# A transformer block on one core: the causal mask of diagonal score units added by a matmul instead of VectorE

## The chip, the core and the metric

The kernel runs on one core of one Trainium2 chip. The metric is device time in microseconds (us) of one execution. The engines are TensorE (PE; PEld is its weight load), VectorE (DVE), ScalarE (ACT), GpSimd (POOL) and SyncE (SP, whose queue issues most DMAs).

## The reference

One layer over 2048 positions of width 1024: RMSNorm, a joint projection, a gated mixing branch (A), forgetting attention (B), the output projection, and a feed-forward part with a causal convolution. What the change touches is branch B, 8 heads of dimension 64:

```python
def block(args):
    i, qi, ci = args
    s = jnp.einsum('bhtd,bshd->bhts', qi, k, preferred_element_type=jnp.float32) * scale
    s = s + ci[..., :, None] - c[:, :, None, :]
    qpos = i * Q_BLOCK + jnp.arange(Q_BLOCK)
    s = jnp.where(kpos[None, :] <= qpos[:, None], s, -jnp.inf)
    p = jax.nn.softmax(s, axis=-1)
    return jnp.einsum('bhts,bshd->bthd', p.astype(v.dtype), v)
...
x = x + jnp.concatenate([out_a, out_b], axis=-1) @ w_out[l]
x = x + conv_ffn(rms_norm(x, norm_ffn_g[l]), w_up[l], w_conv[l], b_conv[l], w_down[l])
```

`c` is a cumulative sum of log-sigmoid forget logits. Arithmetic is at float32 accuracy: operands are split in a high and a low fp32r part, and a product is three matmuls.

## The kernel before

Two kinds of work run side by side. The first is the chain of large products, in 512-column tiles: the input projections in two halves of 1024 positions (`a_half`), the output projection of the first half (`c_half`), its up-projection (`d_half`), the output projection of the second half (`c_late`), and then the feed-forward products of the rest (`up_mms`, L1171 to L1173, and `down`, L1373). Up to `c_late` each tile `mm` is a series of 24 matmuls, all at L212 in `mm3`, with `thi`, `tlo` the activations' parts and `whi`, `wlo` the weights'.

The second is attention, a generator (`b_stream`) that is advanced once every few L212 matmuls (`tick`, `RATES`). It goes over 4 query blocks `tb` of 512 and within each over 8 heads `h`. For each pair a first pass (`b_max`, L774 to L784) forms scores and reduces them on VectorE to a maximum per query (`part`), and a second pass (`b_mix`) forms them again, transposed, by unit `sc` of 128 keys: two matmuls into a PSUM tile `s` or `dn` (L821 with keys `m1` and queries `t1`, L822 with `m2` and `t2`), an exponential on ScalarE into `e` (L827), its high part `ph` on ScalarE (L832) and low part `pl` on VectorE (L833), the running sum on VectorE (L835), and two or three units later the product with the values (L809 with `ph`, L810 with `pl`, into `o`). A pair has 4*tb + 4 units. The last 4 are diagonal: unit j of them covers query columns from 128*j on (widths 512, 384, 256, 128), and its first 128 columns get the mask `maskT` on VectorE (L825). After a pair of heads, L851 sums `sum` over the keys, L852 inverts it, `rw` (L857) spreads it, four transposes (L186, `s<-ident,rw`) turn it, L860 scales, and the result goes to DRAM (`mixh`, `mixl`).

`need(tb)` makes the program finish query block tb before the DMAs `thi<-mixh`, `tlo<-mixl` (`load_mix`) bring it to `c_half` or `c_late`: the last chunks of the second projection block of each half (from L212 matmul 2304 of the trace's count in the first half, from 4800 in the second; 36 further ones can run without the last chunks) wait for it. Transposes L186 `dn<-ident,ar` turn rows of the first half for the up-projection.

The order of instructions on every engine is not the order of the code. A scheduler of the framework places each instruction in a simulated run of its own, with priorities (`high_priority` for attention's steps, weights' casts further ahead), so an instruction more or less in attention moves others on all engines. The pools' buffer counts are in `BUFS`: three `s` tiles and, later, two `dn` for scores, two `m2` and `v`, one `t2`.

Of the kernel before, what the change touches and what calls it, by code (L numbers as in the profile page):

```python
# [10 lines left out]
BF16 = mybir.dt.bfloat16  # L11
AF = mybir.ActivationFunctionType
ALU = mybir.AluOpType
# [5 lines left out]
P = 128  # L19
# [6 lines left out]
TB = 512  # L26
EPS = 1e-6
BIG = 1e30
EVEN = 104

# [21 lines left out]
def f32(ap):  # L54
    return ap.bitcast(F32)
# [26 lines left out]
class Block:  # L82
# [589 lines left out]
    def b_consts(self):  # L672
        nc, bp = self.nc, self.bp
        ones = self.til(self.sp, [P, TB], F32, "st")[:2, :]
        nc.gpsimd.memset(ones, 1.0)
        for i in range(2):
            self.dma(self.ones_d[:, i * TB:(i + 1) * TB], ones)
        for k in self.kx:
            self.dma(k[:, 128:130, :], self.ones_d.unsqueeze(0).broadcast_to([8, 2, HALF]))
        self.mask = bp.tile([P, TB], BF16, name="mask")  # L680
        nc.gpsimd.memset(self.mask, 0.0)

        nc.gpsimd.affine_select(out=self.mask, in_=self.mask, compare_op=ALU.is_ge, fill=BIG, base=384,
                                pattern=[[-1, TB]], channel_multiplier=1)

        self.maskT = bp.tile([P, P], BF16, name="maskT")
        bp.tile([P, EVEN], F32, name="even")
        nc.gpsimd.memset(self.maskT, 0.0)
        nc.gpsimd.affine_select(out=self.maskT, in_=self.maskT, compare_op=ALU.is_ge, fill=BIG, base=0,
                                pattern=[[1, P]], channel_multiplier=-1)  # L690

        self.rowsel = bp.tile([8, 4, P], BF16, name="rowsel")
        nc.gpsimd.memset(self.rowsel, 1.0)
        for base, mult in ((0, 1), (1, -1)):
            nc.gpsimd.affine_select(out=self.rowsel, in_=self.rowsel, compare_op=ALU.is_ge, fill=0.0, base=base,
                                    pattern=[[-2 * mult, 4], [0, P]], channel_multiplier=mult)
        self.M1, self.T1 = [[self.til(self.mp, [P, TB], F32R, tag) for _ in range(2)] for tag in ("m1", "t1")]
        for m in self.M1:
            nc.gpsimd.memset(f32(m[64:128, :]), 0.0)
            nc.gpsimd.memset(f32(m[96:104, :]), 1.0)  # L700
        for t in self.T1:
            nc.gpsimd.memset(f32(t[64:128, :]), 0.0)
            self.dma(f32(t[66:68, :]), self.ones_d[:, 0:TB])
# [95 lines left out]
    def b_mix(self, h, tb, t1, t2, turn):  # L799

        nc, bp, pp = self.nc, self.bp, self.bpp
        po = self.til(pp, [P, TB], F32, "o")
        total = self.til(self.mp, [P, TB], F32, "sum")
        ns = 4 * tb + 4
        late = []

        def pv():
            sc, c, v, ph, pl = late.pop(0)
            nc.tensor.matmul(po[:, c], lhsT=v, rhs=ph[:, c], start=sc == 0, stop=False)  # L809
            nc.tensor.matmul(po[:, c], lhsT=v, rhs=pl[:, c], start=False, stop=sc == ns - 1)  # L810

        for sc in range(ns):
            if sc == TURN and turn:
                turn()
            if sc % 4 == 0:
                m1, m2, v4 = self.b_keys(h, sc // 4, True)
            j = max(0, sc - 4 * tb)
            c = slice(j * P, TB)
            ks = slice((sc % 4) * P, (sc % 4 + 1) * P)
            ps = self.scores([P, TB])  # L820
            nc.tensor.matmul(ps[:, c], lhsT=m1[:, ks], rhs=t1[:, c], start=True, stop=False)  # L821
            nc.tensor.matmul(ps[:, c], lhsT=m2[:, ks], rhs=t2[:, c], start=False, stop=True)  # L822
            if sc >= 4 * tb:
                d = ps[:, j * P:(j + 1) * P]
                nc.vector.tensor_tensor(d, d, self.maskT, op=ALU.add)  # L825
            e = self.room([P, TB], F32, "e") if sc else total
            nc.scalar.activation(e[:, c], ps[:, c], AF.Exp, scale=-1.0)  # L827
            if len(late) >= (LAG + 1 if self.more else LAG):
                pv()
            ph = self.room([P, TB], F32R, "ph")  # L830
            pl = self.room([P, TB], F32R, "pl")
            nc.scalar.activation(ph[:, c], e[:, c], AF.Copy)  # L832
            nc.vector.tensor_tensor(pl[:, c], e[:, c], f32(ph[:, c]), op=ALU.subtract)  # L833
            if sc:
                nc.vector.tensor_tensor(total[:, c], total[:, c], e[:, c], op=ALU.add)  # L835
            late.append((sc, c, v4[:, sc % 4, :], ph, pl))
            yield
        while late:
            pv()
            yield  # L840

        if h % 2 == 0:
            self.op = self.til(self.mp, [P, TB], F32, "op")
            self.rr = self.til(bp, [P, 4, 2], F32, "rr")
        op = self.op
        own, other = (slice(0, 64), slice(64, 128)) if h % 2 == 0 else (slice(64, 128), slice(0, 64))
        nc.scalar.activation(op[own, :], po[other, :], AF.Copy)
        nc.vector.tensor_tensor(op[own, :], po[own, :], op[own, :], op=ALU.add)
        ps = self.scores([P, 4])
        for i in range(4):  # L850
            nc.tensor.matmul(ps[:, i:i + 1], lhsT=total[:, i * P:(i + 1) * P], rhs=self.mhalf[:, 0:1], start=True, stop=True)  # L851
        nc.vector.reciprocal(self.rr[:, :, h % 2], ps)  # L852
        if h % 2 == 0:
            return

        rw = self.til(self.mp, [P, 4, 2, 64], F32, "rw")
        nc.scalar.activation(rw, self.rr.unsqueeze(3).broadcast_to([P, 4, 2, 64]), AF.Copy, scale=-0.5)  # L857
        yield
        pr = self.transpose4(None, "s", [rw[:, i, :, :].rearrange("p a b -> p (a b)") for i in range(4)])
        nc.vector.tensor_tensor(op, pr, op, op=ALU.mult)  # L860
        oh = self.room([P, TB], F32R, "ph")
        ol = self.room([P, TB], F32R, "pl")
        self.split_sb(op, oh, ol)
        cs = slice(512 + (h - 1) * 64, 512 + (h + 1) * 64)
        self.dma(self.mixh[tb][cs, :], f32(oh))
        self.dma(self.mixl[tb][cs, :], f32(ol))
# [692 lines left out]
```

## Time and profile before

| | |
|---|---|
| median of 3 runs | 2424.99 us (2424.58 to 2426.9) |
| the profiled execution | 2425.66 us, of which the span from first to last instruction is 2424.0 us |
| mean granted clock of TensorE | 0.991 |
| PE busy | 2375.0 us (98%), 11224 matmuls |
| PEld, DVE, ACT, POOL busy | 81%, 78%, 47%, 14% |
| attention | from 142.9 us (first L774) to about 1518 us |

A row of a group has the line, engine, operation, out<-in, shapes and count; then busy us, mean ns of one; then the engine's idle time ahead of it and who ended it. A row of the timeline has start, duration (us), engine, line, operation and what ended idle time in brackets. A row of waits has the total, the number and the longest. Matmuls are pipelined, so the duration of one (0.39 us for 512 columns) is longer than the step from its start to the next one's (0.22 to 0.23).

### The profile page before, as it was taken

Reading aid. Unit: us, or ns where it says so; the run is one execution under the profiler, and the core shown is the slowest. Engines: PE = TensorE matmul, PEld = TensorE weight load, DVE = VectorE, ACT = ScalarE, POOL = GpSimd, SP = SyncE. Lnnn points to the kernel's source line nnn. Section 1 sums busy time; section 2 is a strip of 40 time slices with the busy share of each in tenths; the row PEclk is TensorE's granted clock in tenths of the full one; section 3 lists DMA queues with packets and bytes.
Section 4 is the critical chain, followed back from the end, with each engine's and each line's share of the span. In section 5 each row is a group of like instructions: output and inputs, shape, how many; then the busy total and the mean of one; then the engine's idle time right before and its main releaser. Section 6 shows DMA issues by size and latency. Waiting matters only on the chain.

```text
span 2424.0 us, 32411 instructions
## 1 busy us (share of the span) xinstructions
PE 2375.0 (98%) x11224; PEld 1974.9 (81%) x11224; DVE 1900.7 (78%) x3324; ACT 1150.2 (47%) x1986; POOL 335.8 (14%) x315
## 2 busy tenths in 40 slices
PE   9999999999999999999999999899999999999998
PEld 7888888988778888888887887688888887888887
DVE  5357777866679988999999887598888877957875
ACT  4235655432424444454454435465555455454444
POOL 4114130101123222222222010100000000000001
PEclk9999999999999999999999999899999999999999
DMA  8663536658545444444444453312222228538633
GB/s 263 185 242 99 176 95 175 173 170 294 174 156 195 163 143 152 144 155 148 150 159 151 164 200 132 122 53 88 86 79 87 87 91 308 163 100 299 202 119 123
DMA packets 234517, 379.56 MB, mean 157 GB/s; under 512 B 49944, under 2 KB 109464, under 8 KB 232928
## 3 DMA queue, kind: packets, MB, share of 16 engines
q1 hardware_dynamic: 229312, 353.36, 45.3%
q0 software_dynamic: 5040, 24.12, 2.5%
q8 instruction: 89, 1.46, 0.3%
q14 instruction: 76, 0.62, 0.1%
HBM read 283.82 MB, written 93.72 MB: 156 GB/s over the span
## 4 chain that ended last, share of the span: by engine, by line
PE 83%; DVE 6%; DMA 5%; issue 3%; ACT 1%; POOL 1%; SPq 0%; POOLq 0%; DVEq 0%; ACTq 0%
PE mm L212 39%; PE D L1373 14%; PE A L1171 3%; PE A L1172 3%; PE A L1173 3%; PE o L810 2%; PE o L809 2%; PE s L774 2%; PE s L822 2%; PE s L821 2%; PE B L1172 2%; PE B L1173 2%; PE B L1171 2%; DVE sum L835 1%; PE C L1171 1%
## 5 line engine op out<-in xcount | busy, mean ns | idle before, releaser
L212 PE MATMUL mm<-tlo,whi 128*128 128x512 f32 x896 | 352.4, 394 | 0.0
L212 PE MATMUL mm<-thi,whi 128*128 128x512 f32 x896 | 351.9, 393 | 0.5 <-DVE vn L520 0.5
L212 PE MATMUL mm<-thi,wlo 128*128 128x512 f32 x896 | 352.0, 393 | 0.0
L212 PE MATMUL mm<-whi,thi 128*128 128x512 f32 (+2 forms) x768 | 279.3, 364 | 16.3 <-DMA thi<-mixh 9.0
L212 PE MATMUL mm<-wlo,thi 128*128 128x512 f32 (+2 forms) x768 | 277.3, 362 | 2.0 <-DVE wlo L165 2.0
L212 PE MATMUL mm<-whi,tlo 128*128 128x512 f32 (+2 forms) x768 | 275.8, 360 | 0.4 <-DMA tlo<-mixl 0.4
L151 POOL TENSOR_SCALAR whi<-raw 128x1024 fp32r<-128x1024 f32 (+3 forms) x114 | 144.3, 1267 | 915.0 <-PE mm L212 743.0
L212 PEld LDWEIGHTS mm<-thi,whi 128*128 128x128 f32 x896 | 168.6, 188 | 34.5 <-issue 0.7
L212 PEld LDWEIGHTS mm<-tlo,whi 128*128 128x128 f32 x896 | 168.6, 188 | 33.6
L212 PEld LDWEIGHTS mm<-thi,wlo 128*128 128x128 f32 x896 | 168.6, 188 | 33.1
L212 PEld LDWEIGHTS mm<-whi,thi 128*128 128x128 f32 x768 | 146.9, 191 | 37.6 <-DMA thi<-mixh 10.0
L835 DVE TENSOR_TENSOR sum<-sum,e 128x512 f32<-128x512 f32 (+3 forms) x249 | 161.7, 650 | 13.6 <-ACT e L827 10.6
L212 PEld LDWEIGHTS mm<-wlo,thi 128*128 128x128 f32 x768 | 147.2, 192 | 22.5 <-DVE wlo L165 2.9
L212 PEld LDWEIGHTS mm<-whi,tlo 128*128 128x128 f32 x768 | 146.7, 191 | 21.8 <-DMA tlo<-mixl 1.3
L165 DVE TENSOR_TENSOR wlo<-raw,whi 128x1024 fp32r<-128x1024 f32 (+2 forms) x106 | 131.5, 1241 | 33.7 <-POOL whi L151 33.4
L827 ACT ACTIVATE e<-s 128x512 f32<-128x512 f32 (+3 forms) x207 | 105.2, 518 | 108.5 <-DVE s L825 46.9
L1373 PE MATMUL D<-wl,xh 128*128 128x512 f32 x368 | 141.5, 389 | 0.0
L1373 PE MATMUL D<-wh,xh 128*128 128x512 f32 x368 | 140.8, 389 | 0.2 <-DVE xo L1474 0.2
L833 DVE TENSOR_TENSOR pl<-e,ph 128x512 fp32r<-128x512 f32 (+3 forms) x195 | 123.5, 637 | 21.1 <-PE o L810 13.9
L1373 PE MATMUL D<-wh,xl 128*128 128x512 f32 x368 | 137.7, 389 | 0.0
L832 ACT ACTIVATE ph<-e 128x512 fp32r<-128x512 f32 (+3 forms) x195 | 105.4, 549 | 46.1 <-PE o L809 39.1
L931 ACT ACTIVATE a<-mm 128x512 f32<-128x512 f32 x88 | 52.6, 598 | 122.3 <-PE mm L212 118.3
(1837 smaller groups left out, 5756.4 us busy)
## 6 DMA issues: line engine op xcount, KB each, us to landing
raw<-in_w_up_dram SPq DMA_DIRECT2D x72, 512.0 KB
m<-kx SPq DMA_DIRECT2D x160, 136.0 KB
x<-act SPq DMA_DIRECT2D x84, 256.0 KB
m<-kx SPq DMA_DIRECT2D x67, 256.0 KB
v<-vd SPq DMA_DIRECT2D x67, 256.0 KB
raw<-in_w_in_dram SPq DMA_DIRECT2D x28, 512.0 KB
raw<-in_w_out_dram SPq DMA_DIRECT2D x24, 512.0 KB
tw<-in_w_down_dram SPq DMA_DIRECT2D x11, 1024.0 KB
```

The lines of the kernel that those rows point to most:

```text
L151: self.cast_ins = self.nc.gpsimd.tensor_scalar(out, in_, 1.0, 0.0, ALU.mult, ALU.add).ins
L165: nc.vector.tensor_tensor(lo, raw, f32(hi), op=ALU.subtract)
L212: self.last_mm = self.nc.tensor.matmul(ps, lhsT=a[k], rhs=b[k], start=i == 0, stop=i == 3 * n - 1).ins
L827: nc.scalar.activation(e[:, c], ps[:, c], AF.Exp, scale=-1.0)
L832: nc.scalar.activation(ph[:, c], e[:, c], AF.Copy)
L833: nc.vector.tensor_tensor(pl[:, c], e[:, c], f32(ph[:, c]), op=ALU.subtract)
L835: nc.vector.tensor_tensor(total[:, c], total[:, c], e[:, c], op=ALU.add)
L931: nc.scalar.activation(a[:, 2:TB + 2], ps, AF.Copy)
L1171: mm(ps, lhsT=xh[:, ks], rhs=yh[:, k, :], start=fresh and k == 0, stop=False, **kw)
L1172: mm(ps, lhsT=xh[:, ks], rhs=yl[:, k, :], start=False, stop=False, **kw)
L1173: mm(ps, lhsT=xl[:, ks], rhs=yh[:, k, :], start=False, stop=k == 3, **kw)
L1373: nc.tensor.matmul(bank[t], lhsT=x[i][:, ts], rhs=w[k], start=fresh and j == 0 and i + k == 0, stop=last and i == 1, **kw)
```

## The change

The mask of a diagonal unit is added inside the accumulation: between L821 and L822 a matmul with a bfloat16 unit matrix `same` as weights and the bfloat16 `maskT` as moving operand adds it to the unit's first 128 columns of PSUM. The VectorE addition is gone. `same` is made once, by a ScalarE copy of `ident` that stands at the head of ScalarE's order. The padding tile `even` shrinks by as many bytes as `same` takes, so other tiles keep their addresses.

```diff
-EVEN = 104
+EVEN = 40
...
+        self.same = bp.tile([P, P], BF16, name="same")
+        nc.scalar.activation(self.same, self.ident, AF.Copy)
...
             nc.tensor.matmul(ps[:, c], lhsT=m1[:, ks], rhs=t1[:, c], start=True, stop=False)
+            if sc >= 4 * tb:
+                nc.tensor.matmul(ps[:, j * P:(j + 1) * P], lhsT=self.same, rhs=self.maskT, start=False, stop=False,
+                                 skip_group_check=True)
             nc.tensor.matmul(ps[:, c], lhsT=m2[:, ks], rhs=t2[:, c], start=False, stop=True)
-            if sc >= 4 * tb:
-                d = ps[:, j * P:(j + 1) * P]
-                nc.vector.tensor_tensor(d, d, self.maskT, op=ALU.add)
```

In the new program lines behind the edits stand a little lower: the two score matmuls, L821 and L822, are L824 and L828 there, the mask L826, the value products, L809 and L810, are L812 and L813, and L774 and L851 are L777 and L854.

Three places show how the scheduler's order moves. All are TensorE's rows.

The first is a head of query block 1, late in it, whose second pass begins. Before, its first two units (tiles `s_5194`, `s_5210`) follow close behind the end of the head ahead, L822 right behind L821:

```order
L821 MATMUL s_5194<-t_49_401,m_48_400 128x512
L810 MATMUL o_4946<-pl_5091,v_5059 128x384
L809 MATMUL o_4946<-ph_5117,v_5059 128x256
L821 MATMUL s_5210<-t_49_401,m_48_400 128x512
L822 MATMUL s_5210<-t_1174_5185,m_1177_5190 128x512
L822 MATMUL s_5194<-t_1174_5185,m_1177_5190 128x512
L212 MATMUL mm_6854<-wlo_6550,thi_6158 128x512
```

Now the head starts earlier against the L212 matmuls, and 28 of these stand between a third L821 and the L822 of all three units:

```order
L813 MATMUL o_4948<-pl_5141,v_5061 128x128
L824 MATMUL s_5236<-t_49_403,m_48_402 128x512
L212 MATMUL mm_6437<-wlo_6342,thi_6161 128x512
...
L212 MATMUL mm_6492<-wlo_6342,thi_6161 128x512
L828 MATMUL s_5212<-t_1174_5187,m_1177_5192 128x512
L828 MATMUL s_5196<-t_1174_5187,m_1177_5192 128x512
L828 MATMUL s_5236<-t_1174_5187,m_1177_5192 128x512
```

Further loads of L212 work thus stand ahead of the first matmul that needs `t2`, `m2` of the new head.

The second is the end of query block 1. Before, the last values products, the `rw` transposes, other transposes and the first-pass scores of block 2 stand in one piece of 46 rows without an L212, right after the last L212 that can run without block 1:

```order
L809 MATMUL o_5187<-ph_5354,v_5277 128x128
L186 MATMUL dn_7144<-ident,ar_6647 128x128
...
L810 MATMUL o_5187<-pl_5355,v_5277 128x128
L186 MATMUL s_5435<-ident,rw_5421 128x128 x4
L774 MATMUL s_6351<-m_48_400,t_50_402 128x512
L774 MATMUL s_6359<-m_48_400,t_50_402 128x512
L186 MATMUL dn_7171<-ident,ar_6647 128x128
```

Now the same transposes come 57 L212 matmuls ahead of that point, and L212 rows follow at once:

```order
L813 MATMUL o_5189<-pl_5357,v_5279 128x128
L186 MATMUL s_5437<-ident,rw_5423 128x128 x4
L777 MATMUL s_6353<-m_48_402,t_50_404 128x512
L777 MATMUL s_6361<-m_48_402,t_50_404 128x512
L212 MATMUL mm_6856<-whi_6551,thi_6160 128x512
L212 MATMUL mm_6856<-wlo_6552,thi_6160 128x512
```

So block 1 ends earlier against the products, and what stood in one piece stands between them.

The third is the end of attention. Before, 85 matmuls of attention in one piece, units of the last two heads, follow the last L212 that can run without block 3; they begin with

```order
L212 MATMUL mm_15131<-whi_14875,tlo_14853 128x512
L810 MATMUL o_12972<-pl+_3050_13172,v+_3034_13116 128x512
L809 MATMUL o_12972<-ph+_3055_13193,v_13183 128x512
L821 MATMUL dn_13334<-t_49_401,m_48_400 128x512
L822 MATMUL dn_13334<-t_3076_13291,m_3079_13296 128x512
```

Now it is 17, the last products and sums of the last head alone:

```order
L212 MATMUL mm_15133<-whi_14877,tlo_14855 128x512
L813 MATMUL o_13295<-pl+_3143_13518,v_13461 128x512
L812 MATMUL o_13295<-ph+_3148_13538,v_13528 128x512
...
L812 MATMUL o_13295<-ph+_3163_13597,v_13528 128x128
L854 MATMUL s_13625<-mhalf,sum_13296 128x1
L813 MATMUL o_13295<-pl+_3164_13598,v_13528 128x128
L186 MATMUL dn_13636<-ident,rw_13631 128x128 x4
L212 MATMUL mm_15087<-whi_14883,thi_14853 128x512
```

The units that were in that piece now stand between earlier L212 rows. On SP's queue the loads of attention keep their sequence within a head but move with it.

## The prediction

> **What bounds the kernel now.** I read the page's busy times and its chain first, then the waits of TensorE (PE), then a table of stretches.
>
> ```profile
> PE 2375.0 (98%) x11224; PEld 1974.9 (81%) x11224; DVE 1900.7 (78%) x3324; ACT 1150.2 (47%) x1986; POOL 335.8 (14%) x315
> PE 83%; DVE 6%; DMA 5%; issue 3%; ACT 1%; POOL 1%; SPq 0%; POOLq 0%; DVEq 0%; ACTq 0%
> PE mm L212 <- DMA thi<-mixh: 9.0, 2, 7.2
> PE o L810 <- DVE pl L833: 4.0, 6, 1.2
> PE s L822 <- DMA v<-vd: 3.2, 1, 3.2
> PE s L774 <- DVE part L777: 2.9, 4, 1.0
> 625.00:641.00 16.00, 12.79 (x52) 10.35 (x51) 5.11 (x13) 5.83 (x13) 4.03 (x6) 0.79 0.73 215
> 641.00:655.00 14.00, 14.00 (x71) 11.62 (x70) 9.19 (x18) 7.72 (x14) 1.86 (x3) 1.00 0.62 190
> 655.00:680.00 25.00, 19.14 (x81) 12.56 (x80) 18.96 (x40) 7.22 (x14) 0.00 (x0) 0.80 0.35 107
> 900.00:1200.00 300.00, 298.84 (x1371) 247.72 (x1370) 275.90 (x522) 140.47 (x258) 67.08 (x54) 1.00 0.46 151
> 1495.00:1515.00 20.00, 17.78 (x66) 10.73 (x66) 18.01 (x35) 16.84 (x32) 0.00 (x0) 0.91 0.17 54
> 1515.00:1532.00 17.00, 8.40 (x32) 6.31 (x32) 4.72 (x10) 10.16 (x15) 3.49 (x8) 0.60 0.50 181
> ```
>
> TensorE is 98% busy and 83% of the chain, so what it gains or loses is the time. The waits say where it is not full: few places, and the long ones are singles. The stretches (columns: span, PE, PE weight loads, DVE, ACT, POOL, granted clock, DMA share, GB/s) show them. In 641 to 655 us PE is full, 71 matmuls in 14 us at clock 1.00. In 625 to 641, 655 to 680 and from 1495 it has fewer matmuls and clocks of 0.60 to 0.91: these are the places where the first product stream (`mm`, L212) has run into data that attention has not delivered. Elsewhere, as in 900 to 1200 us, PE is 99.6% busy and VectorE (DVE) 92%.
>
> **The cost: 128 more matmuls.** There are 32 pairs of head and query block with 4 diagonal units each: 128. Each unit gets a 128-column matmul and its weight load between L821 and L822. Such a bfloat16 matmul stands nowhere in this trace. The nearest rows are the 128-column matmuls among 512-column ones:
>
> ```profile
> 641.50 0.39 PE L212 MATMUL mm<-whi,tlo 128*128 128x512 f32 x1
> 641.72 0.22 PE L809 MATMUL o<-ph,v 128*128 128x128 f32 x1
> 641.78 0.45 PE L212 MATMUL mm<-whi,thi 128*128 128x512 f32 x1
> 642.07 0.22 PE L810 MATMUL o<-pl,v 128*128 128x128 f32 x1
> ...
> 649.18 0.22 PE L821 MATMUL s<-t,m 128*128 128x128 f32 x1
> 649.24 0.27 PE L822 MATMUL s<-t,m 128*128 128x128 f32 x1
> 649.35 0.45 PE L212 MATMUL mm<-whi,thi 128*128 128x512 f32 x1
> 649.63 0.39 PE L212 MATMUL mm<-wlo,thi 128*128 128x512 f32 x1
> ```
>
> The durations overlap, so starts are what counts. From 641.50 to 641.72 a 512-column matmul takes its 0.22 to 0.23 us. The short one at 641.72 is followed after 0.06, but the next long one then takes 0.29 (641.78 to 642.07): short and long together 0.35, so the short one costs 0.12. Where two short ones stand together (649.18 to 649.63, 0.45 us with the long one) the second adds 0.10. I take 0.115 us each, wide or narrow unit: 128 x 0.115 = 14.7 us. The low end is the 0.06 alone: 7.7 us. The high end is a matmul that overlaps nothing, its full 0.22: 28.2 us. I stay with 14.7 because the disturbed neighbour after it is again an fp32r one, as in these rows. The Trainium skill, "TensorE: Matmul & The Clock Gate", section on the back-to-back issue gap, gives about 81 ns for each 128-column matmul with its weight load; by that the sum would be 10.4 us.
>
> **What goes.** VectorE loses 128 additions:
>
> ```profile
> L825 DVE TENSOR_TENSOR s<-s,maskT x108: 277/290/332, 160.8 to 1508.8; 128x128 f32<-128x128 f32 x108
> L825 DVE TENSOR_TENSOR dn<-dn,maskT x20: 279/286/293, 952.3 to 1506.6; 128x128 f32<-128x128 f32 x20
> ```
>
> 128 x 0.29 = 37 us of VectorE, nearly all beside a full PE: worth nothing directly. It shortens the way from scores to exponential on diagonal units, since ScalarE no longer queues behind VectorE's backlog. The one copy that makes `same` stands ahead of ScalarE's first split and I cost it at nothing: if ScalarE's work there were late, it would be one copy, under 0.3 us.
>
> **What moves, and why I expect a gain.** The order on every engine changes from the first diagonal unit on; the pieces ahead of this section show that attention stands earlier against L212. That matters at three places.
>
> Place 1, about 631 us:
>
> ```profile
> 631.32 0.40 PE L821 MATMUL s<-t,m 128*128 128x512 f32 x1
> 634.92 1.19 PE L822 MATMUL s<-t,m 128*128 128x512 f32 x2 [3.21 <-DMA v<-vd]
> ...
> 640.18 0.41 PE L212 MATMUL mm<-whi,tlo 128*128 128x512 f32 x1
> ```
>
> PE starts nothing between 631.32 and 634.92, where 0.23 was due: 3.4 us. Then 12 matmuls (2 of L822, 10 of L212) take until 640.18, 5.26 us instead of 12 x 0.23 = 2.8: 2.5 us at the low clock. Together 5.9. In the new order 28 matmuls of L212 stand ahead of this head's first L822, 6.4 us of cover against a wait of 3.2. I count all of it, 5.9.
>
> Place 2, the end of query block 1:
>
> ```profile
> 654.78 0.38 PE L186 MATMUL dn<-ident,ar 128*128 128x128 f32 x2
> ...
> 660.70 0.66 PE L186 MATMUL s<-ident,rw 128*128 128x128 f32 x4 [0.17 <-ACT rw L857]
> ...
> 673.98 0.79 PE L212 MATMUL mm<-whi,thi 128*128 128x512 f32 x1 [1.87 <-DMA thi<-mixh]
> ```
>
> ```profile
> L774 PE MATMUL s<-m,t 96*128 96x512 f32 x12 | 6.7, 598 | 1.8 <-DVE part L777 1.7
> L186 PE MATMUL dn<-ident,ar 128*128 128x128 f32 x27 | 4.2, 277 | 0.4 <-DVE tlo L196 0.3
> ```
>
> The second fence has the two largest groups of that stretch: 12 first-pass scores and 27 transposes, beside which only some 20 rows of L212 stand. Of all matmuls that start between 655 and 680 us, 34 have 512 columns (34 x 0.23 = 7.8 us), 29 are transposes at 0.11 apart (from 654.78: two end 0.38 after the first start, one lasts 0.27; 3.2 us) and 15 are narrower (3 of 384, 3 of 256, the rest shorter, about 1.7 us): 12.7 us of work in 25, 12.3 lost. Here all L212 work that needs no result of block 1 is used up before the last heads' tail, and transposes and first-pass scores then queue behind VectorE. In the new order 57 matmuls of L212 follow the `rw` transposes before the first that needs the last chunks: 13 us of full PE. At the end of attention, in the rows of place 3, the same way from `rw` to L212 takes 8.3 us (1517.79 to 1526.09). So it is covered; I count 11, keeping 1.3 for the slow part that has other causes.
>
> Place 3, the end of attention:
>
> ```profile
> 1508.79 0.29 DVE L825 TENSOR_TENSOR s<-s,maskT 128x128 f32<-128x128 f32 x1
> ...
> 1514.98 0.31 PE L810 MATMUL o<-pl+_3164_13596,v 128*128 128x128 f32 x1
> ...
> 1517.79 1.12 PE L186 MATMUL dn<-ident,rw 128*128 128x128 f32 x4 [1.22 <-ACT rw L857]
> 1526.09 0.79 PE L212 MATMUL mm<-whi,thi 128*128 128x512 f32 x1 [7.18 <-DMA thi<-mixh]
> ```
>
> Between 1495 and 1515 us PE starts 65 matmuls, 45 of them wide (10.4 us), 4 of 384 and 4 of 256 (1.2), 12 shorter (0.7): 12.3 of 20, 7.7 lost to the pace of VectorE (18.0 of 20 busy). Before, 85 attention matmuls follow the last L212 that can run without the result; now 17 do, the rest stand between L212 rows. Four of the removed additions lie here as well, those of the last head's diagonal units, the last at 1508.79: 1.2 us. The last head is still worked off one unit after another, so I count 5 of the 7.7. The tail after 1514.98 stays: nothing in the new order covers the 7.2 us for the last `thi`.
>
> New waits in a denser order, and small waits that the lighter VectorE saves, I let cancel but for 1 us of new ones: the four rows of waits above other than the named stops amount to a few us in all.
>
> **Sum.** 14.7 - 5.9 - 11 - 5 + 1 = -6.2 us, and with the rounding of the low clock at place 3 (PE enters the final wait at full clock, so the 1.2 us of L851 and L186 there shrink) about -7.5. The profiled execution took 2425.66 us (span 2424.0 and 1.7 around it), 0.7 above the median of the three runs, 2424.99. I predict 2417.5 us.
>
> **Rivals.** (a) Only place 2 is repaired: a load is late elsewhere in place of that at 631, and the last head again runs at VectorE's pace. For it: SP's order of loads moves as well, and the cover of head 7's first L822 is as short in the new order as before. Then 14.7 - 11 - 1 = +2.7: 2428, no difference that can be told.
> (b) Slower: PE is the full engine, it gets 14.7 us more, and the stops re-form, because they come from one mechanism, VectorE's rate: each unit asks it for a difference and a sum, and a new order does not change that. Then only the four additions and part of place 1 are won, about 3: 2437. It decides when less than 9.8 us of the 24 lost at the three places come back (14.7 less the 4.9 that are 0.2%, what a measurement of this kernel can tell from no change). Against it: VectorE is idle 6.0 of the 25 us of place 2 (18.96 busy), so that stop is order, not rate. The Trainium skill, "Perfetto Trace Analysis", optimization strategy, says to work on the most contended engine, and by that rule moving work onto PE loses; the trace agrees that PE is that engine, but also shows it waiting.
> (c) The short matmul costs 0.06 only: 7 us less than the forecast, 2410.5.
>
> **Chances.** Forecast 0.58 (own range 2410 to 2422), (a) 0.22, (b) 0.12, (c) 0.08. The range reaches from (c) with place 3 whole, 2408, over (a) to 2431, which leaves out (b) and the high price. Faster by over 0.2%, below 2420.1: nine tenths of the forecast and (c), 0.61. Within 0.2%: 0.27. Slower: 0.12.
>
> **What would show it.** Right: the waits of L822 on a DMA (3.2) and of L774 on `part` (2.9) go, that on `thi` falls from 9.0 in 2 to about 7 in 1; the stretch of 25 us at clock 0.80 near 660 us is full; the run of attention alone before 1518 us is short; a masked unit's L821 to the matmul after L822 takes 0.115 us longer. Wrong: start to start steps of 0.2 us around the mask matmul, or PE waits on `e`, `pl` and loads scattered from 150 to 1500 us that amount to over 5 us.

## The result and the profile after

The changed kernel takes 2422.64 us (median of 20 runs, 2418.44 to 2425.25) against 2425.18 for the kernel before (20 runs). The ratio is 0.9986, interval 0.998 to 0.9993: 0.14% faster, or 1.7 to 4.9 us. The interval lies wholly below 1, so the gain is real, but it is under the 0.2% that the prediction took as the bound of a difference. The time lies inside the predicted range (2408 to 2431), 5 us above the predicted 2417.5: a third of the forecast gain of 7.5 us came. The profiled execution took 2422.66 us, with a span of 2420.9.

From the page, busy times and chain, and from the waits of TensorE (total, number, longest, us):

```profile
PE 2379.3 (98%) x11352; PEld 1973.2 (82%) x11352; DVE 1881.9 (78%) x3196; ACT 1152.9 (48%) x1987; POOL 331.3 (14%) x315
PE 79%; DVE 5%; DMA 2%; issue 2%; ACT 2%; POOL 1%; SPq 0%; POOLq 0%; DVEq 0%; ACTq 0%
PE mm L212 <- DMA thi<-mixh: 8.8, 2, 7.3
PE o L813 <- DVE pl L836: 4.5, 4, 2.8
PE mm L212 <- DMA tlo<-mixl: 1.3, 1, 1.3
```

128 matmuls more, 128 VectorE instructions less. The waits of the second score matmul on a DMA (3.2) and of the first pass on `part` (2.9) are gone; `thi` still has two waits, the long one as before, and that for `tlo` has grown from 0.4 to 1.3. The same stretches as before (columns: span, PE, weight loads, DVE, ACT, POOL, granted clock, DMA share, GB/s), and two more of both kernels behind them:

```profile
625.00:641.00 16.00, 16.00 (x79) 13.07 (x78) 13.51 (x18) 8.01 (x16) 4.64 (x5) 1.00 0.69 223
655.00:680.00 25.00, 22.17 (x110) 17.77 (x109) 11.97 (x26) 4.55 (x8) 1.86 (x3) 1.00 0.46 143
1495.00:1515.00 20.00, 18.67 (x94) 15.07 (x92) 17.08 (x31) 12.82 (x26) 0.00 (x0) 0.98 0.14 47
1515.00:1532.00 17.00, 9.26 (x36) 7.16 (x36) 6.21 (x10) 8.94 (x13) 3.49 (x8) 0.62 0.59 216
690.00:800.00 110.00, 106.17 (x499) 86.72 (x498) 93.24 (x154) 50.07 (x91) 37.45 (x33) 0.98 0.56 187
```

```profile
690.00:800.00 110.00, 108.79 (x515) 90.01 (x514) 98.38 (x165) 50.09 (x91) 40.29 (x35) 1.00 0.60 202
```

The three stops have filled: 79 matmuls against 52 in 625 to 641 us, 110 against 81 in 655 to 680, 94 against 66 in 1495 to 1515. The tail of the end (1515 to 1532) is the old one. From 690 to 800 us, where it stood almost full before, TensorE now starts 16 matmuls fewer.

**Where the time went.** TensorE sets the time, so I took the step from each matmul's start to the next one's and subtracted what a plain row of that width takes (0.227 us for 512 columns, 0.175, 0.12 and 0.06 for 384, 256 and 128). What is left is lost time; what stands at a mask matmul (its own step, and the delay of the one behind it) is counted apart, without four waits of 0.2 to 0.6 us that fall on such a place. In us, from the two traces:

| stretch | lost before | lost after | at mask matmuls |
|---|---|---|---|
| 0 to 150, ahead of attention | 15.8 | 13.4 | 0 |
| 150 to 600 | 28.4 | 32.9 | 6.7 |
| 600 to 690, places 1 and 2 | 21.9 | 7.0 | 1.0 |
| 690 to 800 | 5.6 | 9.6 | 1.0 |
| 800 to 1490 | 20.3 | 18.0 | 6.5 |
| 1490 to 1600, place 3 | 28.1 | 19.9 | 0.5 |
| 1600 to the end | 2.7 | 3.1 | 0 |
| sum | 122.8 | 103.9 | 15.7 |

103.9 + 15.7 - 122.8 = -3.2, the difference of the spans (2420.9 - 2424.0 = -3.1). The matmuls cost 15.7, the three places gave 23.1 (14.9 + 8.2), and 8.5 were lost anew from 150 to 600 and from 690 to 800 us. The 2.4 ahead of attention stand in unchanged code and are a difference between two executions. Two runs below show how far one trace can be trusted, since each repeats an order up to 800 us: the changed order with mask matmuls of one column loses 30.6, 6.6 and 11.1 us in the three rows from 150 to 800, and the old order in a second kernel 28.8, 22.6 and 5.5. So a row carries some 1 to 2 us of chance, and of the 4.5 us lost anew from 150 to 600 more than half may be chance.

A masked unit in the timeline (start, duration; TensorE):

```profile
1043.59 0.39 PE L212 MATMUL mm<-thi,wlo 128*128 128x512 f32 x1
1043.82 0.39 PE L824 MATMUL dn<-t,m 128*128 128x512 f32 x1
1044.05 0.23 PE L826 MATMUL dn<-maskT,same 128*128 128x128 bf16 x1
1044.09 0.48 PE L828 MATMUL dn<-t,m2+_2078_9223 128*128 128x512 f32 x1
1044.40 0.34 PE L824 MATMUL s<-t,m 128*128 128x384 f32 x1
```

The mask matmul is followed after 0.04 us, but the wide one behind it takes 0.31 to 0.32 instead of 0.23. From L824 to the matmul behind L828 it is 0.585 us in the median of 21 such units, against 0.454 for two such rows without a mask (median of 185 in the kernel before): 0.13 for the mask. In units of 256 and 384 columns it is 0.13 too, in those of 128 about 0.08 (0.245 against 0.170).

### The profile page after: what moved, and what is told of

It is laid out like the page before. It is cut to its first block, busy times and chain, and to the rows that moved or that the text cites. A ratio compares the mean times of both kernels' runs of the same rounds, so it can differ in the third digit from the quotient of the medians.

```text
span 2420.9 us, 32633 instructions
## 1 busy us (share of the span) xinstructions
PE 2379.3 (98%) x11352; PEld 1973.2 (82%) x11352; DVE 1881.9 (78%) x3196; ACT 1152.9 (48%) x1987; POOL 331.3 (14%) x315
## 4 chain that ended last, share of the span: by engine, by line
PE 79%; DVE 5%; DMA 2%; issue 2%; ACT 2%; POOL 1%; SPq 0%; POOLq 0%; DVEq 0%; ACTq 0%
PE mm L212 35%; PE D L1376 13%; PE A L1174 3%; PE A L1176 3%; PE A L1175 3%; PE o L813 3%; PE o L812 2%; PE s L777 2%; PE s L828 2%; PE s L824 2%; PE B L1175 2%; PE B L1176 2%; PE B L1174 2%; PE C L1174 1%; PE C L1175 1%
## 5 line engine op out<-in xcount | busy, mean ns | idle before, releaser
L212 PE MATMUL mm<-thi,wlo 128*128 128x512 f32 x896 | 352.9, 394 | 0.0
L212 PE MATMUL mm<-thi,whi 128*128 128x512 f32 x896 | 352.1, 393 | 0.5 <-DVE vn L520 0.5
L212 PE MATMUL mm<-tlo,whi 128*128 128x512 f32 x896 | 352.5, 393 | 0.0
L212 PE MATMUL mm<-whi,thi 128*128 128x512 f32 (+2 forms) x768 | 277.4, 362 | 14.3 <-DMA thi<-mixh 8.8
L212 PE MATMUL mm<-wlo,thi 128*128 128x512 f32 (+2 forms) x768 | 276.7, 361 | 1.9 <-DVE wlo L165 1.8
L212 PE MATMUL mm<-whi,tlo 128*128 128x512 f32 (+2 forms) x768 | 275.4, 360 | 1.3 <-DMA tlo<-mixl 1.3
L151 POOL TENSOR_SCALAR whi<-raw 128x1024 fp32r<-128x1024 f32 (+3 forms) x114 | 135.2, 1187 | 909.3 <-PE mm L212 665.9
L212 PEld LDWEIGHTS mm<-thi,whi 128*128 128x128 f32 x896 | 168.8, 188 | 34.5 <-issue 0.9
L212 PEld LDWEIGHTS mm<-tlo,whi 128*128 128x128 f32 x896 | 168.8, 188 | 33.9
L212 PEld LDWEIGHTS mm<-thi,wlo 128*128 128x128 f32 x896 | 168.9, 188 | 33.2
L838 DVE TENSOR_TENSOR sum<-sum,e 128x512 f32<-128x512 f32 (+3 forms) x249 | 163.6, 657 | 20.8 <-ACT e L830 18.2
L212 PEld LDWEIGHTS mm<-whi,thi 128*128 128x128 f32 x768 | 146.1, 190 | 35.8 <-DMA thi<-mixh 9.6
L212 PEld LDWEIGHTS mm<-wlo,thi 128*128 128x128 f32 x768 | 146.1, 190 | 22.5 <-DVE wlo L165 3.1
L212 PEld LDWEIGHTS mm<-whi,tlo 128*128 128x128 f32 x768 | 146.0, 190 | 21.4 <-DMA tlo<-mixl 1.7
```

The lines of the kernel that those rows point to most:

```text
L151: self.cast_ins = self.nc.gpsimd.tensor_scalar(out, in_, 1.0, 0.0, ALU.mult, ALU.add).ins
L212: self.last_mm = self.nc.tensor.matmul(ps, lhsT=a[k], rhs=b[k], start=i == 0, stop=i == 3 * n - 1).ins
```

## The experiments

Two theories. **Theory O**: the change costs its price on TensorE, and what it wins is the order that the scheduler happened to draw; the 37 us of VectorE are worth nothing. **Theory V**: the stops come from VectorE's load, and its relief removed them. Times are compared with runs of the kernel before on the same chip; its medians there were 2423.8 to 2426.4.

### One column instead of 128

```diff
-                nc.tensor.matmul(ps[:, j * P:(j + 1) * P], lhsT=self.same, rhs=self.maskT, start=False, stop=False,
+                nc.tensor.matmul(ps[:, j * P:j * P + 1], lhsT=self.same, rhs=self.maskT[:, 0:1], start=False, stop=False,
```

> The changed kernel with the mask matmul cut to 1 of its 128 columns (so most of the mask is left out, and the exponential's scale is 0.01 to keep it finite). The instruction order on TensorE is that of the changed kernel row for row until attention has ended. Theory W, the price of a mask matmul is that of one more instruction and its weight load: the steps around it stay at 0.039 and 0.316 us where they are now, about 0.12 us more than two matmuls without it, and the time stays at 2422 within 3 us. Theory C, the price is its 128 columns: the two steps shrink to those of a plain pair, 12 of the 14.2 us go, 2410.

2423.33 us, ratio to the kernel before 0.9996 (0.9988 to 1.0005): no gain against 128 columns.

```profile
1044.22 0.39 PE L824 MATMUL dn<-t,m 128*128 128x512 f32 x1
1044.45 0.18 PE L826 MATMUL dn<-maskT,same 128*128 128x1 bf16 x1
1044.49 0.48 PE L828 MATMUL dn<-t,m2+_2078_9223 128*128 128x512 f32 x1
1044.81 0.33 PE L824 MATMUL s<-t,m 128*128 128x384 f32 x1
```

The same steps, 0.23, 0.04, 0.32; a unit takes 0.588 us in the median of 21. Theory W holds: here the columns cost nothing, the instruction does.

### The unit matrix as fp32r

```diff
-        self.maskT = bp.tile([P, P], BF16, name="maskT")
+        self.maskT = bp.tile([P, P], F32R, name="maskT")
...
-        self.same = bp.tile([P, P], BF16, name="same")
+        self.same = bp.tile([P, P], F32R, name="same")
```

> The changed kernel with the unit matrix and the mask as fp32r instead of bfloat16 (the order forms anew, without a long piece at either place). In the run with one column the price did not move, so the weight load is the suspect: a bfloat16 load takes 0.096 us, an fp32r one 0.188. Theory L (the price is the load): a masked 512-column unit takes 0.585 + 0.09 us, 128 x 0.09 = 11.8 us more, 2434. Theory I (the price is a fixed one for any instruction more): 0.585 stays and the time stays at 2423 within 5.

2410.27 us, ratio 0.9945 (0.9932 to 0.9958), which neither theory of the price gave: the order formed anew. So the price is read from the steps. The weight loads of the mask in this kernel and in the changed one (duration ns min/median/max):

```profile
L826 PEld LDWEIGHTS s<-maskT,same x108: 187/188/193, 158.0 to 1486.3; 128*128 128x128 f32 x108
```

```profile
L826 PEld LDWEIGHTS <-same x128: 95/96/100, 157.5 to 1506.0; 128*128 128x128 bf16 x128
```

The load takes twice as long, and a masked 512-column unit 0.576 us (median of 20) against 0.585. Theory L is wrong there: the load's duration is not the price. Only in the narrowest units, of 128 columns, does the longer load show (0.282 us against 0.245). Over all 128 units the two masks cost the same (15.9 against 15.7 us), so the 12 us against the changed kernel are put down to the order: the two waits on `thi` are both absent from its list of waits, and the place-3 stretch loses 7.1 us instead of 19.9. Its last `rw` transposes stand at L212 number 4780, 56 ahead of the last product that can run without attention's result.

### A unit matrix of 32 columns

```diff
-                nc.tensor.matmul(ps[:, j * P:(j + 1) * P], lhsT=self.same, ...
+                nc.tensor.matmul(ps[0:32, j * P:(j + 1) * P], lhsT=self.same[:, 0:32], ...
```

> The changed kernel with a unit matrix of 32 columns instead of 128 as weights, so that only 32 of a unit's 128 rows of keys get the mask (most of the mask is left out, the exponential's scale is 0.01). The order is that of the changed kernel everywhere. Theory L2 (the load's time goes with the columns loaded): the bfloat16 load falls from 0.096 to 0.03 or so and the masked 512-column unit from 0.585 to about 0.52: 2414. Theory I (fixed): 0.585 and 2423.

2442.05 us, ratio 1.0075 (1.0062 to 1.0088): some 20 us slower than the changed kernel, which neither theory gave.

```profile
L826 PEld LDWEIGHTS <-same x128: 91/92/95, 158.0 to 1527.4; 128*32 128x32 bf16 x128
1057.44 0.39 PE L824 MATMUL dn<-t,m 128*128 128x512 f32 x1
1057.76 0.23 PE L826 MATMUL dn<-maskT,same 128*32 128x128 bf16 x1
1057.92 0.50 PE L828 MATMUL dn<-t,m2+_2078_9223 128*128 128x512 f32 x1
1058.25 0.34 PE L824 MATMUL s<-t,m 128*128 128x384 f32 x1
```

A quarter of the columns load in 0.092 us instead of 0.096, and each change between the shapes 128*128 and 128*32 costs more: the step to the mask matmul is 0.32 us instead of 0.23, its own 0.16 instead of 0.04, and the unit takes 0.81 instead of 0.585.

### No mask at all

```diff
-            if sc >= 4 * tb:
-                d = ps[:, j * P:(j + 1) * P]
-                nc.vector.tensor_tensor(d, d, self.maskT, op=ALU.add)
```

> The kernel before without any mask in the second pass (left out, exponential's scale 0.01), so neither VectorE's 128 additions nor TensorE's matmuls. The order forms anew: the 49 attention matmuls in one piece near L212 number 2412 are gone, and 64 instead of 85 stand in one piece at the end of attention. Theory O (order decides, VectorE's 37 us are worth nothing): stops at 631 to 680 us gone, -20, the end keeps about 5 of its 7.7, new small waits +4: about 2407. Theory V (VectorE's load makes the stops): the same place gains plus the scattered waits on VectorE, 2400 or less. If the stops stay although the order has changed: 2425.

2418.19 us, ratio 0.9971 (0.996 to 0.9983), less gain than either theory gave. The loss from 600 to 690 us falls from 21.9 to 5.0, as expected; but it rises by 4.9 from 150 to 600 and by 5.1 from 690 to 800, and the end, 64 rows in one piece, loses 25.6 against 28.1. Against V: VectorE is relieved of all 128 additions and TensorE of all mask matmuls, yet it is slower than the fp32r kernel above, which keeps the matmuls, and than two kernels below that keep the additions.

### The mask twice

```diff
+            if sc >= 4 * tb:
+                d = ps[:, j * P:(j + 1) * P]
+                nc.vector.tensor_tensor(d, d, self.maskT, op=ALU.add)
             e = self.room([P, TB], F32, "e") if sc else total
```

> The changed kernel with VectorE's 128 additions kept beside the 128 mask matmuls (the mask added twice, which leaves the result). VectorE carries its full former load and TensorE the new one. The order has the 49-row piece near L212 number 2412 gone, but 87 attention matmuls in one piece at the end. Theory O: before + 14.2 (matmuls) - 17 (631 to 680 us) + 4 (new small waits), the end as before: about 2426. Theory V (the stop near 660 us is made by VectorE's load): it stays, 2440.

2431.12 us, ratio 1.0032 (1.002 to 1.0045). 5 above Theory O's figure, 9 below V's. Its stretches:

```profile
655.00:680.00 25.00, 22.31 (x108) 18.23 (x107) 14.54 (x30) 4.80 (x7) 0.55 (x1) 0.93 0.31 101
1500.00:1520.00 20.00, 16.53 (x60) 10.49 (x59) 18.29 (x35) 15.44 (x30) 0.00 (x0) 0.86 0.12 41
```

With VectorE's full load the stop near 660 us is gone all the same (108 matmuls, changed kernel 110, before 81; loss from 600 to 690 us 8.6 against 21.9). The end, where 87 rows stand in one piece, is as slow as before.

### One place at a time, without the change

Two numbers of the scheduler's tables, one kernel each:

```diff
-RATES = [3.5, 4.0, 4.4, 3.6]
+RATES = [3.5, 4.0, 5.2, 3.6]
```

> The kernel before with one number changed, RATES[2] 5.2 for 4.4: TensorE's order is the old one up to L212 number 3155, and the last piece of attention is 21 rows instead of 85. Theory O: the stops at 631 and 660 us stay as they were, the end gains 6 of its 7.7 us: 2418. If a shorter last piece is worth nothing, because VectorE's work is only done earlier and the wait for the last thi grows by as much: 2424.

2416.29 us, ratio 0.9968 (0.9956 to 0.998), as Theory O gave. From 655 to 680 us TensorE starts 70 matmuls, as slow as before; the loss from 1490 to 1600 falls from 28.1 to 20.8.

```diff
-GATE_LAG = 30
+GATE_LAG = 24
```

> The kernel before with one number changed, GATE_LAG 24 for 30: no instruction more or less. The 49-row piece near L212 number 2412 is gone from TensorE's order; the piece at the end of attention grows from 85 to 147 rows. Theory O (each stop is a matter of the order): about -16 in the stretch that ends with L212 number 2496, as in the changed kernel without its matmuls, and at the end +5, because 62 more rows run at VectorE's pace: 2414. Theory V (the stop near 660 us is VectorE's load, which is untouched): the stretch stays, 2424 to 2430.

2439.3 us, ratio 1.0057 (1.0046 to 1.0069): a miss. The stretch up to L212 number 2496 is 17 us shorter, as expected, but about 8 of these are attention's work that has only moved behind it; the loss from 600 to 690 us falls from 21.9 to 11.8. And the last piece of 147 rows costs far more than the 5 that I scaled from 85: from 800 to 1600 us it loses 64.9 against 48.4.

```profile
1480.00:1500.00 20.00, 15.67 (x53) 10.59 (x52) 15.07 (x31) 13.32 (x25) 0.00 (x0) 0.82 0.35 106
1500.00:1520.00 20.00, 18.10 (x64) 12.58 (x64) 15.49 (x30) 14.99 (x29) 0.00 (x0) 0.83 0.28 89
1520.00:1540.00 20.00, 9.69 (x32) 6.08 (x33) 12.46 (x25) 14.38 (x26) 3.49 (x8) 0.71 0.24 85
PE dn L821 <- DMA m<-kx: 2.6, 2, 2.1
```

Attention alone puts 53 and 64 matmuls into 20 us, with VectorE busy 15 of 20, and loads of `m` come late on top. Either number is no change of work, and each moves the time by 8 to 15 us.

### Both places, without the change

```diff
-RATES = [3.5, 4.0, 4.4, 3.6]
+RATES = [3.5, 4, 10, 4.4]
...
-GATE_LAG = 30
+GATE_LAG = 24
```

> The kernel before, VectorE's mask additions and all, with two tables changed that only move the order: GATE_LAG 24 for 30 and RATES [3.5, 4, 10, 4.4] for [3.5, 4.0, 4.4, 3.6]. Neither long piece of attention is left on TensorE (the longest is 20 rows at the end). Theory O: what the change won was the order, so it is to be had without the matmul: -20 at the places of 631 to 680 us, -6 at the end, +4 small waits: about 2403, faster than both. Theory V: VectorE's rate makes the stops form again as scattered waits: 2418 to 2425.

2410.41 us, ratio 0.9943 (0.9931 to 0.9956): 14 us faster without the matmul, 7 less than expected. The loss from 600 to 690 us falls from 21.9 to 6.2 and that from 1490 to 1600 from 28.1 to 20.8; 5.6 come back from 150 to 600 and from 690 to 800. The tail with its wait for `thi` stays. The fp32r run had lost that wait, with 56 products between the last `rw` and the product that needs the result, so the next kernel has RATES [3.5, 4.0, 20, 4], which makes them 55:

> The kernel before, VectorE's mask additions and all, with GATE_LAG 24 for 30 and RATES [3.5, 4.0, 20, 4] for [3.5, 4.0, 4.4, 3.6]. On TensorE the last transposes of rw of query block 1 follow L212 number 2322 (before: 2340, the last that can run without the block), those of block 3 number 4781 (before and in the changed kernel: 4836, the last), so 55 products, 12.5 us, stand between the end of attention and the first product that needs it. Theory O: the wait for thi of about 7.5 us goes too, as it did in the fp32r run, where that number was 4780: 2410.4 of the reordered kernel less 7.5, 2403, the fastest. If the wait is only moved (VectorE has to do the same work in a shorter time): 2410.

2396.69 us, ratio 0.9889 (0.9876 to 0.9903): 27 us faster than the kernel before, some 24 faster than the changed one by the ratios, and the fastest of all. Its stretches and waits:

```profile
655.00:680.00 25.00, 22.77 (x108) 18.48 (x107) 17.04 (x33) 4.01 (x6) 3.49 (x3) 0.93 0.31 97
1480.00:1505.00 25.00, 25.00 (x125) 20.84 (x124) 10.25 (x18) 11.33 (x17) 3.90 (x8) 1.00 0.62 202
1505.00:1530.00 25.00, 24.49 (x119) 20.30 (x117) 16.11 (x23) 5.11 (x9) 3.98 (x3) 1.00 0.34 116
PE o L810 <- DVE pl L833: 5.8, 5, 2.2
PE mm L212 <- DMA thi<-mixh: 2.2, 1, 2.2
```

The end of attention runs at full clock, and the wait of 7.2 us on the last `thi` does not exist: 55 products cover it.

### The change in the settled order

The same two tables in the changed kernel:

> The changed kernel with the same two tables as the covered kernel before (GATE_LAG 24, RATES [3.5, 4.0, 20, 4]), so that the change is measured where neither kernel has a long piece of attention at the two block ends: the last rw transposes stand at L212 numbers 2247 and 4690 (2322 and 4781 in the covered kernel before). Theory O: what is left of the change is its price, 15.7 us of TensorE by the steps (0.123 us each), against nothing for VectorE's 37 us; 2396.7 + 15.7, less some 3 us for the shorter thi wait at block 1: 2410, slower than the covered kernel before. Theory V: VectorE's 37 us take the waits for pl away (5.8 us there) and more, which pays for the matmuls: 2396 to 2402.

2408.93 us, ratio 0.993 (0.9916 to 0.9943); by the ratios 0.9930 - 0.9889 = 0.41%, 10 us slower than without the change. With the intervals of both ratios that is 5 to 15 us. The spans of the two traces differ by 16.0 (2411.1 against 2395.1), about the 15.5 of the mask matmuls; but that execution of the changed kernel was the slowest of its five, so the medians count. Where neither kernel has a long stop, the change is a loss, as Theory O gave, and Theory V's 2396 to 2402 is out. Whether the loss is the whole price, or a few us of it are paid back by VectorE, these runs do not tell; the orders of the two kernels differ as well (the last `rw` transposes at L212 numbers 4690 and 4781).

### The new stop at 726 us

In the changed kernel the longest of the new waits is one chain over three engines:

```profile
723.93 1.49 POOL L151 TENSOR_SCALAR whi<-raw 128x1024 fp32r<-128x1024 f32 x1
725.38 3.50 POOL L992 TENSOR_TENSOR tw<-tw 128x512 f32<-128x512 f32 x2
725.45 2.31 DVE L165 TENSOR_TENSOR wlo<-raw,whi 128x1024 fp32r<-128x1024 f32 x1 [0.94 <-POOL whi L151]
727.68 1.74 DVE L836 TENSOR_TENSOR pl<-e,ph 128x512 fp32r<-128x512 f32 x1
729.48 0.80 PE L813 MATMUL o<-pl,v 128*128 128x512 f32 x1 [2.80 <-DVE pl L836]
```

```diff
-            tt(out, a, b, op=ALU.subtract)
+            tt(out[:, 0:1], a[:, 0:1], b[:, 0:1], op=ALU.subtract)
```

> The changed kernel with GpSimd's subtractions of the down-projection's weights (L992, tile tw) cut to one column, so that most of these sums are left out. TensorE's order is that of the changed kernel up to L212 number 2601, which is where it stops for 3.0 us at 726 us. Theory P (that new stop is a chain through GpSimd: its cast whi stands behind two tw subtractions, VectorE's wlo waits for the cast, pl stands behind wlo, L813 waits for pl): the stop at 726 shrinks to under 0.5 us. Theory V2 (VectorE has only a backlog of its own from the end of block 1): it stays near 3 us. The total, 2418 by the first, says less, since the order behind it moves.

The stop (the step less 0.227) falls from 2.96 us to 1.36, by 1.6 of the 2.5 that Theory P gave. The run with one column, which has the same order, has it at 3.28. The total, 2407.08 us (ratio 0.9932, 0.9918 to 0.9945), holds a new order behind this point and less work on GpSimd, so it is not put down to the chain.

```profile
724.03 1.22 DVE L165 TENSOR_TENSOR wlo<-raw,whi 128x1024 fp32r<-128x1024 f32 x1 [2.52 <-POOL whi L151]
725.17 0.68 DVE L836 TENSOR_TENSOR pl<-e,ph 128x512 fp32r<-128x512 f32 x1
718.10 2.08 POOL L911 TENSOR_SCALAR ar<-acc,rstd 128x1024 f32<-128x1024 f32 x1
722.13 0.76 POOL L993 DMA_DIRECT2D tw<-tw  x1 [0.31 <-POOL tw L992]
722.93 1.06 POOL L151 TENSOR_SCALAR whi<-raw 128x1024 fp32r<-128x1024 f32 x1
```

VectorE still waits 2.52 us for the cast, with `pl` behind `wlo`, so the end of the chain is the right one. Its first link is not: the cast now ends only 0.33 us before TensorE's last start ahead of the stop, against 0.87 in the changed kernel, because the scaling of a row (`ar`, 2.08) and the issue of a DMA (0.76) stand ahead of it on GpSimd. What the small subtractions took away is length: `wlo` takes 1.22 us instead of 2.31 and `pl` 0.68 instead of 1.74, 2.15 together. Less the 0.54 by which the cast is later, that is 1.6, the whole gain. So the `tw` subtractions held TensorE up by running beside `wlo` and `pl`, not by standing ahead of the cast.

## Why the prediction was right and where it was not

The measured time lies in the range because the range reached up to rival (a); of the gain a third came, and "within 0.2%", which it was, had a chance of 0.27. So most of the mechanism held, and one term of the sum did not.

- **The price**, 14.7 us: 15.7 by the steps, 0.123 each against 0.115. The steps of fp32r neighbours in the trace of before told it. The Trainium skill, "TensorE: Matmul & The Clock Gate", back-to-back issue gap, gives 81 ns, by which an estimate is 10.4 us in all; the trace here does not agree. Rival (c), 0.06, is out.
- **The three places**, 5.9 + 11 + 5 and 1.3 for the clock, 23.2: they gave 14.9 + 8.2 = 23.1. That the sums agree is luck. Places 1 and 2 gave 2.0 less than 16.9: the first product that needs the new data is L212 number 2331, so 48 products cover the way and not 57, and the way from the first `rw` transpose to the product that waits for `thi` takes 15.0 us (648.62 to 663.67), not the 8.3 that were read off place 3; TensorE waits 1.48 us for `thi` (663.67) and 1.35 for `tlo` (667.00). That the waits on `thi` would fall to one was thus wrong too. Place 3 gave about 8 where 5 were counted: from 1495 to 1515 us 8.2 were lost before, and now 0.6 up to the last L212 product that can run (1510 us). The 1.3 for the clock did not come: the tail behind these two points loses 19.8 us up to 1600, before 19.5.
- **New waits, +1**: this step failed. I let new waits and VectorE's relief cancel. From 150 to 600 and from 690 to 800 us 8.5 us were lost anew, from 800 to 1490 2.3 were won: +6.2. What the prediction named as a sign of being wrong is there: the waits on `pl` and on loads come to 7.5 us (5.6 and 1.9), over the 5 that it allowed. The part from 690 to 800, right behind the filled stop at 660 us, is no chance of one trace: the ten that filled the stop, wholly or in part, lose 8.2 to 11.4 us there, the two that kept it 5.5 and 5.6. So 3 to 6 us of what places 1 and 2 gave were handed back within 100 us. The traces show part of the reason: what VectorE did during the stop is still to do. When L212 number 2496 starts, VectorE has been busy 486.9 us in the kernel before, and 474 to 476 in four such kernels that keep all its additions. That this work makes the new waits is argued, not shown: in the changed kernel VectorE is no busier from 690 to 800 us than before (93.2 us against 98.4). The one cause that a run shows is that of the stop at 726 us, GpSimd's subtractions beside VectorE's instructions; with these cut to one column the loss from 690 to 800 us is 5.4, though the order behind 726 us moved as well. The rest of the 8.5 (150 to 600 us) consists of some ten waits of 0.3 to 1.1 us on different things; their cause stays open.
- **VectorE's 37 us, worth nothing directly**: right. With the mask twice VectorE does all of them, and the stop near 660 us is gone; in the settled order their removal does not pay for the matmuls (a loss of 5 to 15 us). That it pays nothing at all is not shown.
- **Rival (b)**, stops that form again from VectorE's rate, did not come: 23 us came back, where it needed less than 9.8. The 24 us that it calls lost at the three places are 25.9 by the prediction's own terms (5.9 + 12.3 + 7.7), and "faster" comes to 0.60 by its chances, not 0.61; neither slip changes the forecast. Rival (a), 2428, is out too, though a difference under 0.2% was the outcome, by small waits and not by a place that stayed.
- The sum of the traces: -7.5 as predicted, +5.2 for the new waits, +1.0 for the price, +0.4 behind 1600 us, -2.4 ahead of attention, +0.1 at the places: -3.2. Without the 2.4, which are no effect of the change, the error is larger than the medians show.

## What to carry to other kernels

Where a scheduler sets the order, an edit that puts one instruction in or out draws a new order. Here orders of the same matmuls and VectorE instructions ran from 27 us faster to 15 us slower than the kernel before, more than the edit's own price of 15.7; judge the edit by running both kernels in an order that has no long stop, as was done with the two tables. Look for the number of independent products between the end of a block and the first that needs it: at the end of attention 55 or more of them removed a wait of 7 us (three kernels), 10 left 4.7 of it, and where none stood there the whole wait stayed. And do not count a filled stop as all won: what ran on the other engines during the stop has to run somewhere.

## What the runs showed of the hardware

- An inserted matmul of one column costs what one of 128 columns costs (0.588 and 0.585 us for the masked unit of 512 columns), and a weight load of 0.188 us costs no more there than one of 0.096 (0.576): about 0.13 us for the instruction between wide fp32r matmuls, most of it paid by the wide matmul behind it (0.32 us instead of 0.23). In units of 128 columns the longer load does cost more (0.282 against 0.245).
- Weights of 32 columns instead of 128 load in nearly the same time (0.092 against 0.096 us) and make the unit 0.23 us longer (0.814), 0.09 of it ahead of the matmul and the rest behind it.
- VectorE's `wlo` of 1024 columns took 2.31 us when one of GpSimd's `tw` subtractions of 512 columns was running as it began, and 1.22 when these had one column. The changed kernel's trace has 100 such `wlo`. Nine began while a large GpSimd instruction (`tw`, a cast, a scaling or `vn`) had 0.61 to 1.23 us still to run, and each took that rest and 1.07 to 1.08 us more. The other 91 took 1.21 to 1.23, also the 13 during which a GpSimd instruction started; among them are two that began beside a small GpSimd instruction, of 4 and of 16 columns, with 0.95 and 2.83 us left to run. The Trainium skill, "SBUF — State Buffer", section "SBUF: two separate sides", says that a VectorE instruction with two SBUF inputs and a GpSimd one that reads SBUF exclude each other from a shared port pair, which the one that starts first holds for its whole instruction; the nine and the 13 agree, the two small ones do not show it.
